# Attention weights times values on one core: the tile context is closed and compiled inside the kernel, and the wait for the last stores stands behind its closing barriers

## The chip, the cores and the metric

The kernel runs on one core of a Trainium2 chip. The metric is the device time of one execution in microseconds (us), as the median of several runs. A second source is the profile of one execution: it gives a span (from the first to the last instruction of the program) and every instruction's and transfer's time in it.

## The reference

```python
def setup_inputs():
    batch, n_heads, seq, head_dim = 8, 12, 1024, 64
    return {
        "attn_weights": np.random.randn(batch, n_heads, seq, seq).astype(np.float32),
        "v": np.random.randn(batch, n_heads, seq, head_dim).astype(np.float32),
    }

def reference(attn_weights, v):
    return np.einsum('bhqs,bhsd->bhqd', attn_weights, v).astype(np.float32)
```

There are 96 heads. For each, a 1024x1024 matrix of weights is multiplied with a 1024x64 matrix of values.

## The kernel before, in words

The 96 heads are taken four at a time, which makes `NV` = 24 groups (`q`), and each group is done in two units, so `NU` = 48 units (`n`). One unit holds 16 rows of weights per partition: the 128 partitions are four heads times 32 blocks of rows.

The steps of a unit, each on its engine, are written out by hand in one critical section with semaphores of their own:

- GpSimd (POOL) issues the load of a unit's weights, 4 MB of them, into one of two buffers `abf`; the transfer casts to bf16. It also loads `v`, several groups at once, and issues most of the stores (`load_attn`, `load_v`, `store`).
- TensorE (PE) transposes the weights (`transpose_g`, line 143), spreads the values over the partitions (`spread_v`, line 160), multiplies (`multiply`, line 188) and transposes the product back (`transpose_back`, line 173).
- VectorE (DVE) and ScalarE (ACT) copy the results of these steps from PSUM (lines 249, 257, 276 and 288). The finished rows go into `osb`, a ring of slots in SBUF from which they are stored.
- SyncE (SP) passes on semaphores and issues the last three stores.

The stores are grouped. Those of the first groups go out in two bursts (`BURSTS`). From `HELD_FROM` = 14 on, POOL holds two stores of 2 MB back until all loads are issued; they count on `s_held`. SP issues three more of 2 MB (`q` = 18, 20 and 22 from `BY_SYNC` = 18 on), which count on `s_end`; each adds 16 when it has landed, 48 in all.

How the program ends is what matters here. Inside the critical section ScalarE waits for `s_held`, and POOL closes its own list with a drain (line 402). The section's own end (line 135) lets all engines go on once POOL is through. Behind it, still inside the tile context, ScalarE waits for `s_end` (lines 433 and 434):

```python
        landed = nc.scalar.alloc_register("landed")
        nc.scalar.reg_mov(landed, 16 * (NV - BY_SYNC) // 2)
    tc.keep_in_program_order(nc.scalar.wait_ge(s_end, nc.scalar.snap(landed)))
    tc.keep_in_program_order(nc.scalar.sem_inc(s_end, 1))
```

When the `with` block of the tile context is left (line 460), the context is closed and compiled, and its closing is appended to every engine's list: a barrier of all five engines, POOL's clear of all the context's semaphores as one range, and a second barrier. In a barrier each engine drains and counts itself on one semaphore; POOL waits until the other four have done so (it gathers) and then lets them go through another semaphore (it releases).

Of the kernel before, what the change touches and what calls it, by code (L numbers as in the profile page):

```python
# [10 lines left out]
def kernel(  # L11
# [18 lines left out]
    nc = tc.nc  # L30
# [18 lines left out]
    NV = NH // VH  # L49
# [4 lines left out]
    BY_SYNC = NV - 6  # L54
# [37 lines left out]
    PER_DVE = sum(on_dve(g) for g in range(G))  # L92
    PER_ACT = G - PER_DVE

    sem = tc.alloc_semaphore
    sb = lambda name, shape, dt: nc.alloc_sbuf_tensor(name, shape, dt).ap()
    ident = sb("ident", [P, P], fp32)
# [18 lines left out]
    s_second = {n: sem(f"s_second{n}") for n in range(HALVED, NU)}  # L116
    s_v0, s_v, s_cast = sem("s_v0"), sem("s_v"), sem("s_cast")
    s_osb = sem("s_osb")
    s_held, s_end = sem("s_held"), sem("s_end")

    s_t = {True: sem("s_t_dve"), False: sem("s_t_act")}
    s_sp, s_m = sem("s_sp"), sem("s_m")
# [12 lines left out]
    with tc.tile_critical(sync_engine=mybir.EngineType.Pool, no_gpsimd_drain=True):  # L135
# [218 lines left out]
        def store(q, fours, eng, done, ready=None):  # L354
            eng.wait_ge(s_out, ready or 2 * (q + fours) + 1)
            at_slot = osb[:, ds(slot(q), fours // 2)].rearrange("p n r d -> p n (r d)")
            eng.dma_start(  # L357
                out=out_n(q, fours), in_=at_slot,
                **({"single_packet": True} if eng is pool and fours == 2 else {}),
            ).then_inc(done, 16)  # L360
# [67 lines left out]
            store(q, 2, nc.sync, s_end)  # L428
        nc.sync.wait_ge(s_fin, 2)
        store(NV - 2, 2, nc.sync, s_end, NU)  # L430
        landed = nc.scalar.alloc_register("landed")
        nc.scalar.reg_mov(landed, 16 * (NV - BY_SYNC) // 2)
    tc.keep_in_program_order(nc.scalar.wait_ge(s_end, nc.scalar.snap(landed)))
    tc.keep_in_program_order(nc.scalar.sem_inc(s_end, 1))


# [28 lines left out]
```

## Time and profile before

| what | value |
|---|---|
| time, median of 3 runs | 1051.74 us (1051.55 to 1052.11) |
| span of the profiled execution | 1049.7 us |
| time less span | 2.04 us |
| moved between HBM and the core | 427.82 MB read, 25.17 MB written |
| busy share of the span | PE 76%, DVE 37%, ACT 45%, POOL 4% |

The profile has no time of its own for the whole execution beside the span, so the profiled execution is set against the median of the runs by the 2.04 us that lie outside the span. In the profile, lines named PE, DVE, ACT and POOL are work of the engines; ACTq, DVEq, POOLq, PEldq and SPq are their sequencers, which execute semaphore instructions, drains, register moves and branches. For a group of instructions of one line it gives the duration in ns (least, median and most), and the start of the first and of the last of them in us from the start of the span. "DMA to landing" is the time from the issue of a transfer until its last part has counted on its semaphore.

### The profile page before, as it was taken

The page shows a single profiled execution, that of the slowest core. Times are in us where ns is not written, and L with a number is a line of the kernel's source. Part 1 is how long each engine was busy: PE and PEld are TensorE (multiplying, and loading weights), DVE is VectorE, ACT ScalarE, POOL GpSimd, SP SyncE. Part 2 cuts the span into 40 slices and gives each one's busy share as a digit, 9 for nine tenths or more (in the row PEclk, how much of TensorE's full clock was granted, in tenths as well). Part 3 has the DMA queues.
Part 4 walks back from the last instruction along what each step waited for, and adds up shares of the span by engine and source line. Part 5 has one row for each costly group of instructions (what it writes and reads, how often), then busy time and mean ns, then how long its engine had stood idle before and what let it go on. Part 6 is the DMA issues. An engine that isn't in the chain of part 4 may idle for free.

```text
span 1049.7 us, 17364 instructions
## 1 busy us (share of the span) xinstructions
PE 799.7 (76%) x7304; PEld 712.2 (68%) x7304; DVE 389.3 (37%) x584; ACT 469.5 (45%) x590; POOL 36.9 (4%) x68
## 2 busy tenths in 40 slices
PE   0978789479789492887949879858578894988984
PEld 0777678478678482777848678647567784877874
DVE  1443344235334251343424344324224341533542
ACT  0445355345445361344535455344335443544643
POOL 1000000000000000000000000000000000000100
PEclk9989889799898796889879989889879987889997
DMA  9999999999999999999999999999999999999999
GB/s 216 225 219 219 217 211 215 220 220 217 219 219 209 216 220 380 217 219 219 206 219 220 220 217 219 207 222 215 327 233 217 219 206 219 219 220 220 209 220 390
DMA packets 10662, 239.68 MB, mean 228 GB/s; under 512 B 1056, under 2 KB 1056, under 8 KB 1184
## 3 DMA queue, kind: packets, MB, share of 16 engines
q0 software_dynamic: 10080, 232.26, 98.8%
q1 hardware_dynamic: 576, 7.34, 1.7%
q8 instruction: 3, 0.05, 0.0%
q14 instruction: 3, 0.02, 0.0%
HBM read 427.82 MB, written 25.17 MB: 432 GB/s over the span
## 4 chain that ended last, share of the span: by engine, by line
DMA 71%; PE 26%; issue 1%; POOL 1%; ACT 0%; DVE 0%; ACTq 0%; SPq 0%; POOLq 0%
DMA abf<-in_attn_weights_dram 63%; PE bank L143 22%; DMA out_dram<-osb 8%; PE bank L160 3%; PE bank L188 1%; PE bank L173 0%; POOL vr L349 0%; ACT osb L257 0%; DVE osb L257 0%; ACT vbf L249 0%; POOL abf L343 0%; ACT ot L288 0%; POOL out_dram L357 0%; ACTq L257 0%; SPq L419 0%
## 5 line engine op out<-in xcount | busy, mean ns | idle before, releaser
L143 PE MATMUL bank<-ident,abf 128*128 128x128 f32 x3072 | 432.8, 309 | 206.3 <-DMA abf<-in_attn_weights_dram 183.1
L143 PEld LDWEIGHTS bank<-ident,abf 128*128 128x128 f32 x3072 | 423.1, 212 | 218.0 <-DMA abf<-in_attn_weights_dram 190.5
L276 DVE COPY at<-bank 128x1024 bf16<-128x1024 bf16 x480 | 319.6, 688 | 399.3 <-PE bank L143 398.5
L276 ACT COPY at<-bank 128x1024 bf16<-128x1024 bf16 x288 | 287.9, 1012 | 326.1 <-PE bank L143 326.1
L188 PE MATMUL bank<-at,vbf 128*64 128x256 bf16 x3072 | 227.3, 286 | 0.0
L188 PEld LDWEIGHTS bank<-at,vbf 128*64 128x64 bf16 x3072 | 204.8, 112 | 20.0 <-issue 6.5
L257 ACT COPY osb<-bank 64x512 f32 (+1 forms) x194 | 112.4, 580 | 28.3 <-PE bank L173 25.7
L288 DVE COPY ot<-bank 128x512 f32<-128x512 f32 x48 | 33.2, 691 | 210.2 <-PE bank L188 210.2
L160 PE MATMUL bank<-vr,spread 32*128 32x512 bf16 x768 | 87.0, 375 | 0.5 <-issue 0.2
L288 ACT COPY ot<-bank 128x512 f32<-128x512 f32 x48 | 28.1, 585 | 132.1 <-PE bank L188 132.1
L173 PE MATMUL bank<-ident,ot 128*128 128x128 f32 x392 | 62.6, 312 | 29.4 <-ACT vbf L249 28.7
L173 PEld LDWEIGHTS bank<-ident,ot 128*128 128x128 f32 x392 | 51.3, 159 | 41.5 <-ACT vbf L249 40.5
L160 PEld LDWEIGHTS bank<-vr,spread 32*128 32x128 bf16 x768 | 35.2, 93 | 43.9 <-issue 1.6
L249 ACT CAST vbf<-bank 128x512 bf16<-128x512 f32 x48 | 25.8, 589 | 74.3 <-PE bank L160 74.3
L343 POOL DMA_DIRECT2D abf<-in_attn_weights_dram x50 | 26.9, 538 | 810.9 <-PE bank L143 810.0
L249 DVE CAST vbf<-bank 128x512 bf16<-128x512 f32 x48 | 30.9, 685 | 29.0 <-PE bank L160 29.0
L276 ACT ACT_TABLE_LOAD x12 | 15.4, 1283 | 6.3 <-DMA osb<-in_v_dram 6.1
L349 POOL DMA_DIRECT2D vr<-in_v_dram x6 | 4.0, 674 | 135.9 <-PE bank L160 135.9
L357 POOL DMA_DIRECT2D out_dram<-osb x5 | 3.1, 619 | 7.5 <-ACT osb L257 7.5
L257 DVE COPY osb<-bank 64x512 f32<-64x512 f32 x2 | 1.4, 689 | 3.0 <-PE bank L173 3.0
L324 DVE MEMSET ident<- 128x128 f32 x1 | 0.2, 165 | 6.1 <-DMA osb<-in_v_dram 6.1
L331 DVE CAST vr<-osb 128x1024 bf16<-128x1024 f32 x2 | 2.2, 1136 | 0.0
(9 smaller groups left out, 5.1 us busy)
## 6 DMA issues: line engine op xcount, KB each, us to landing
abf<-in_attn_weights_dram POOLq DMA_DIRECT2D x46, 4096.0 KB, 29.2
vr<-in_v_dram POOLq DMA_DIRECT2D x5, 2048.0 KB, 15.3
out_dram<-osb POOLq DMA_DIRECT2D x1, 8192.0 KB, 40.4
abf<-in_attn_weights_dram POOLq DMA_DIRECT2D x4, 2048.0 KB, 24.6
out_dram<-osb POOLq DMA_DIRECT2D x3, 2048.0 KB, 35.4
out_dram<-osb SPq DMA_DIRECT2D x3, 2048.0 KB, 13.8
out_dram<-osb POOLq DMA_DIRECT2D x1, 4096.0 KB, 42.5
osb<-in_v_dram SPq DMA_DIRECT2D x1, 1024.0 KB, 5.0
```

Source lines behind the costliest of these rows:

```text
L143: last = pe.matmul(out=pt[g % 4][:, k], lhsT=words[:, k], rhs=ident, is_transpose=True, start=(k == 0), stop=(k == KW - 1),)
L160: last = pe.matmul(out=banks[h], lhsT=spread[rows, j, ds(VB - 1 - b, P)], rhs=vr[rows, n // 2, b], start=(b == 0), stop=(b == VB - 1),)
L173: last = pe.matmul(out=px[j0 // 4][:, ds(j * P, P)], lhsT=ot[:, j0 + j], rhs=ident, is_transpose=True, start=(j == 0), stop=(j == 3),)
L188: last = pe.matmul(out=outs, lhsT=vbf[:, 2 * kw + par, h], rhs=at[:, ds(half * GH, GH), kw, ds(h * VP, VP), par], start=(n == 0), stop=(n ...
L249: copy(out=vbf[:, :, h], in_=ps.rearrange("p (k d) -> p k d", k=SB)).then_inc(s_vbf)
L257: last = copy(out=rows[ds(n // 2 % 2 * HP, HP), ds(pp * 2 * G + n % 2 * G, G)].rearrange("p (half j) d -> p j half d", half=2)[:, ds(4 * k ...
L276: ins = copy(out=at[:, g].rearrange("c k j two -> c (k j two)"), in_=bank[g % 4].bitcast(bf16),)
L288: copy(out=ot.rearrange("c j (pp h p) -> c h j pp p", pp=2, h=VH)[:, ds(2 * e, 2)], in_=po[e].rearrange("c (h j p pp) -> c h j pp p", h=2, ...
L331: last = nc.vector.tensor_copy(out=vr_first[:, 0, part], in_=v32[:, part])
L343: pool.dma_start(out=abf[n % 2][:, ds(g0, gn)].rearrange("p g s -> p (g s)"), in_=attn_q[n // 2][:, ds((n % 2 * G + g0) * S, gn * S)],).th ...
L349: pool.dma_start(out=vr[:, ds(q % V_AT_ONCE // 2, fours // 2)].rearrange("p n b x -> p n (b x)"), in_=v_n(q, fours),).then_inc(s_v, 16)
L357: eng.dma_start(out=out_n(q, fours), in_=at_slot, **({"single_packet": True} if eng is pool and fours == 2 else {}),).then_inc(done, 16)
```

## The change

`s_end` is no longer one of the tile context's semaphores but taken from the program itself, so the closing's range clear leaves it alone. The kernel closes and compiles the tile context itself as its last step but one, and so the closing stands in every engine's list there. Then ScalarE waits for the constant 48 on `s_end` and sets the semaphore back to zero. The register, its copy and the increment go. Leaving the `with` block has nothing left to do for the context.

```diff
     PER_ACT = G - PER_DVE
 
+    s_end = nc.alloc_semaphore("s_end")
     sem = tc.alloc_semaphore
...
     s_osb = sem("s_osb")
-    s_held, s_end = sem("s_held"), sem("s_end")
+    s_held = sem("s_held")
...
         nc.sync.wait_ge(s_fin, 2)
         store(NV - 2, 2, nc.sync, s_end, NU)
-        landed = nc.scalar.alloc_register("landed")
-        nc.scalar.reg_mov(landed, 16 * (NV - BY_SYNC) // 2)
-    tc.keep_in_program_order(nc.scalar.wait_ge(s_end, nc.scalar.snap(landed)))
-    tc.keep_in_program_order(nc.scalar.sem_inc(s_end, 1))
+    tc.close()
+    tc.compile()
+    nc.scalar.wait_ge(s_end, 16 * (NV - BY_SYNC) // 2)
+    nc.scalar.sem_clear(s_end)
```

## The prediction

> **What bounds the kernel now.** I read the page first, from the span down to the chain of waits, then the last 26 us in stretches, then line by line the instructions that end the program.
>
> ```profile
> span 1049.7 us, 17364 instructions
> ...
> DMA  9999999999999999999999999999999999999999
> ...
> HBM read 427.82 MB, written 25.17 MB: 432 GB/s over the span
> ...
> DMA 71%; PE 26%; issue 1%; POOL 1%; ACT 0%; DVE 0%; ACTq 0%; SPq 0%; POOLq 0%
> ```
>
> The DMA engines are 90% busy or more in each of the 40 slices and 71% of the chain that ended last is DMA. The kernel is bound by its transfers from end to end, so an edit outside the transfers can only count at the two ends of the span. The change touches the last end. The table by stretches shows it:
>
> ```profile
> core 0: us, PE busy (x) PEld busy (x) DVE busy (x) ACT busy (x) POOL busy (x), PEclk, DMA share, GB/s
> 1024.00:1037.30 13.30, 11.20 (x121) 10.41 (x119) 6.89 (x11) 8.16 (x12) 0.00 (x0) 1.00 1.00 429
> 1037.30:1042.70 5.40, 0.00 (x0) 0.00 (x0) 0.00 (x0) 0.00 (x0) 0.00 (x0) 0.54 1.02 434
> 1042.70:1048.60 5.90, 0.00 (x0) 0.00 (x0) 0.00 (x0) 0.00 (x0) 0.00 (x0) 0.50 0.78 333
> 1048.60:1049.70 1.10, 0.00 (x0) 0.00 (x0) 0.00 (x0) 0.00 (x0) 0.00 (x0) 0.50 0.00 0
> ```
>
> Compute is over at 1037.3. From there to 1048.6 only stores move, and in the last 1.1 us not even those: no engine is busy and no byte flows. What these 1.1 us are is the whole question. The instructions of three lines tell it, first the last store and who waits for it:
>
> ```profile
> L357 SPq DMA_DIRECT2D out_dram<-osb x1: 332/332/332, 1037.3 to 1037.3; - x1
> ...
> DMA to landing us min/median/max: 11.3/11.3/11.3
> ```
>
> ```profile
> L434 ACTq EVENT_SEMAPHORE  x1: 17/17/17, 1048.7 to 1048.7; - x1
> ```
>
> The last of SP's three stores is issued at 1037.3 and lands 11.3 us later, at 1048.6. ScalarE's wait (line 434) starts to execute at 1048.7, once that has landed, and takes 17 ns. The closing of the tile context is line 460; here are its instructions before the landing and after it, in two windows:
>
> ```profile
> L460 SPq EVENT_SEMAPHORE  x3: 17/27/28, 1042.8 to 1043.0; - x3
> L460 SPq DRAIN  x2: 7/7/7, 1043.0 to 1043.1; - x2
> ...
> L460 POOLq DRAIN  x1: 47/47/47, 1043.1 to 1043.1; - x1
> ```
>
> ```profile
> L460 POOLq EVENT_SEMAPHORE  x4: 17/17/17, 1048.8 to 1049.6; - x4
> L460 ACTq DRAIN  x2: 8/8/8, 1048.7 to 1049.0; - x2
> ...
> L460 PEldq EVENT_SEMAPHORE  x2: 51/51/51, 1048.9 to 1049.6; - x2
> L460 POOLq DRAIN  x2: 39/85/131, 1048.9 to 1049.4; - x2
> ...
> L460 POOLq EVENT_SEMAPHORE_RANGE_CLEAR  x1: 268/268/268, 1049.1 to 1049.1; - x1
> ```
>
> SP and POOL reach the first closing barrier at 1043.1 and stand there. ScalarE is the fifth, and it comes only at 1048.7, with its drain behind the wait of line 434. Then the closing runs in the open: POOL gathers (1048.8), releases (PE leaves at 1048.9), drains, clears the range of semaphores (268 ns from 1049.1), drains, gathers and releases again, and the last engine leaves at 1049.6 plus 51 ns, which is the span's end.
>
> **The change part by part.** Nothing ahead of the tail is touched. The loops, the loads, the stores and the order of every queue stay; the sole new fact for the body is that one semaphore is taken outside the tile context, and the trace holds no instruction for taking one. I cost that at nothing.
>
> Removed: the register that held 48 and its copy, both on ScalarE's sequencer.
>
> ```profile
> L432 ACTq MOVE  x1: 29/29/29, 1040.1 to 1040.1; - x1
> ```
>
> ```profile
> L433 ACTq MOVE  x1: 34/34/34, 1042.8 to 1042.8; - x1
> ```
>
> They are 29 and 34 ns, at 1040.1 and 1042.8, so both lie under the 5.9 us for which ScalarE then waits for the landing. Worth nothing; without that cover they would be 0.06 us.
>
> Moved: the wait for the three stores, from ahead of both barriers to behind them. ScalarE then reaches the first barrier without it. What is late next in that barrier is POOL:
>
> ```profile
> L402 POOLq DRAIN  x1: 47343/47343/47343, 995.4 to 995.4; - x1
> ```
>
> ```profile
> L135 POOLq EVENT_SEMAPHORE  x3: 17/43/43, 1042.7 to 1043.0; - x3
> ...
> L135 ACTq DRAIN  x1: 8/8/8, 1042.8 to 1042.8; - x1
> ```
>
> POOL's drain of line 402 runs from 995.4 for 47.3 us, to 1042.7, and the critical section ends behind it, for ScalarE with a drain of 8 ns at 1042.8. POOL itself comes to the closing barrier at 1043.1 and its drain there ends at 1043.2. Behind the last arrival the closing takes what it takes now: from ScalarE's arrival at 1048.7 to 1049.7, 1.0 us. So in the changed kernel the closing runs from 1043.2 to about 1044.2. The cover is the flight of the last store, which lands at 1048.6: 4.4 us are left over. If that cover were gone (a store that landed by 1043.2), the gain would be gone with it. Behind the moved wait on ScalarE only the clear is queued, and no other engine waits for either; no DMA is issued behind it, and no queue of SP or POOL is passed by anything but the closing itself.
>
> What then ends the program is the wait at 1048.7 (17 ns, the same row of line 434 as now) and the clear behind it. Gain so far: 1049.7 - 1048.7 = 1.0 us.
>
> Added: the clear of one semaphore by ScalarE, in place of the increment that today rides on the wait. No such instruction stands in the trace. From below its price is nothing, if it is carried by the waiting instruction as the increment is. From above it is POOL's clear of a whole range, 268 ns. One semaphore is nearer to the 17 ns of ScalarE's other semaphore instructions; with the step from one instruction to the next I take 0.1 us, and keep 0 to 0.3.
>
> Around the span: the median is 1051.74 and the span 1049.7, so 2.04 us lie outside what the profile shows. Four engines are through 4.5 us sooner (at 1044.2 for 1048.7), and only ScalarE is left. Whatever of the 2.04 us these four do on their own ends up hidden; whatever ScalarE does, or all five together, stays. The bounds are 0 and -2.04 us. I take 0, by the nearest row: in the barrier of today four engines stood ready for 5.6 us, and after the fifth the closing still ran its full 1.0 us. The Trainium skill (Runtime: NRT & Kernel Launch, "The ~15µs preamble/postamble breakdown") has the work behind a kernel begin with a barrier that waits for all engines; by that rule the early four gain nothing there and the sum stays as it is. The page's stages around a kernel add up to far more than 2.04 us, so this measured time can't hold all of them, and no run so far shows which it holds.
>
> Sum: -1.0 + 0.1 = -0.9 us on the profiled span, 1049.7 to 1048.8; on the median 1051.74 to 1050.84, say **1050.8**. That is 0.09%. About 0.2%, or 2.1 us, is what a measurement of this kernel can tell from no change, so this forecast counts as "within".
>
> **The rivals.** *Four early engines shorten what lies around the span.* For it: the 2.04 us are unseen, and each engine must have some end of its own. Against it: a program isn't over before its last engine, and that one still has its own end to make. It makes the result faster by over 2.1 us once it hides more than 2.1 - 0.9 = 1.2 of the 2.04 us. With all of it hidden the time is 1050.8 - 2.0 = 1048.8; with 1.2, 1049.6. Less than that stays inside the forecast's class.
>
> *A closing drain holds until the stores have landed.* This is the one that ends slower. POOL's drain of line 402 shows that a drain can hold: the two stores it stands behind were landed when ScalarE's wait for them fired at 1040.1 (the MOVE of line 432 carries that wait), and the drain held until 1042.7, 2.6 us more. In the trace the two drains after the first barrier (131 and 39 ns) run only after the last landing; in the changed kernel they would meet two stores in flight. Should the one ahead of the clear, or SP's in the second barrier, hold in the same way, it ends at 1048.6 + 2.6 = 1051.2, then come the clear, the drain and the second barrier, 1049.7 - 1049.1 = 0.6 us, and the wait and clear, 0.1: 1051.9 for 1049.7, a time of 1053.9, slower by 2.2 us or 0.21%. It decides from a hold of about 2.5 us after the landing; a shorter one eats the gain and no more. Against it: SP's drains at 1043.0 and 1043.1 took 7 ns, and POOL's at 1043.1 took 47 ns, with SP's own store still 5 us from landing.
>
> *The move doesn't take place in the program.* If the wait were still emitted ahead of a barrier, the tail would stay as it is: 1051.7. Against it: the context is compiled on the line before, and what is traced afterwards can only follow.
>
> **How the numbers follow.** The forecast gets 0.62; its own range is 1050.4 to 1051.2: from the clear at 0 to 0.3 us (1050.7 to 1051.0), 0.2 us at the high side and 0.3 at the low for the spread of the runs (1051.55 to 1052.11) and a little hidden around the span. The early engines get 0.27: no row prices the 2.04 us, and four engines in five end sooner. The holding drain gets 0.07: drains of the same kind were seen not to hold. The wait that doesn't move gets 0.04 and counts as within. So faster 0.27, same 0.66, slower 0.07. The range goes from 1048.8, all that the first rival can give, to 1051.3, just over the forecast's own end; outside remain the drain, the unmoved wait and the stray end of a run.
>
> **What would show it.** In the changed profile the closing's instructions, whatever line they then bear, should run from about 1042.8 to 1044.2 with POOL's range clear near 1043.6; ScalarE's wait should start within 0.1 us of the last landing, 11 to 12 us after SP's last store was issued, with at most one instruction behind it; and the span should end 0.1 to 0.3 us after that landing, at about 1048.8 if the stores land as now. If the drains behind the first barrier show microseconds, the second rival is at work. If the median falls by much more than the span, it is the first. The prediction is wrong if a stretch of 1 us without transfers still stands at the end, or if the time moves by over 2 us either way.

## The result, and the profile after

The changed kernel takes 1050.42 us (median of 21 runs, 1050.12 to 1052.04) where the kernel before takes 1051.76 us (21 runs beside them). The ratio is 0.9988, with a 95% interval of 0.9982 to 0.9993: a gain of 1.3 us, or 0.12%. That is less than the 0.2% that the prediction took as the least that can be told from no change, yet the interval stays clear of 1. The profiled execution took 1050.13 us, with a span of 1048.7 us. The forecast was 1050.8.

The last 25 us in stretches, cut at the issue of the last store, at the end of the critical section and at the landing, as before. The columns are each engine's busy time, the granted clock, the share of the DMA engines and what they moved:

```profile
core 0: us, PE busy (x) PEld busy (x) DVE busy (x) ACT busy (x) POOL busy (x), PEclk, DMA share, GB/s
...
1036.90:1042.60 5.70, 0.00 (x0) 0.00 (x0) 0.00 (x0) 0.00 (x0) 0.00 (x0) 0.52 1.01 431
1042.60:1048.60 6.00, 0.00 (x0) 0.00 (x0) 0.00 (x0) 0.00 (x0) 0.00 (x0) 0.50 0.75 322
1048.60:1048.70 0.10, 0.00 (x0) 0.00 (x0) 0.00 (x0) 0.00 (x0) 0.00 (x0) 0.50 0.00 0
```

The stretch without transfers has shrunk from 1.1 us to 0.1. Where the closing went is seen in the instructions of its line, which is 433 now (the line that compiles the context), in the last 7 us:

```profile
L433 SPq EVENT_SEMAPHORE  x5: 17/17/28, 1042.8 to 1044.0; - x5
L433 POOLq EVENT_SEMAPHORE  x4: 17/17/17, 1043.1 to 1043.9; - x4
L433 SPq DRAIN  x3: 7/7/7, 1042.9 to 1043.4; - x3
L433 POOLq DRAIN  x3: 39/47/124, 1043.1 to 1043.8; - x3
...
L433 PEldq EVENT_SEMAPHORE  x2: 51/51/51, 1043.3 to 1044.0; - x2
L433 POOLq EVENT_SEMAPHORE_RANGE_CLEAR  x1: 267/267/267, 1043.5 to 1043.5; - x1
```

All of it lies between 1042.8 and 1044.0, and POOL's three drains and its range clear take what they took before, though stores are in flight. Last come the store, issued at 1036.9 with 11.7 us to its landing at 1048.6, and ScalarE:

```profile
L358 SPq DMA_DIRECT2D out_dram<-osb x1: 333/333/333, 1036.9 to 1036.9; - x1
...
DMA to landing us min/median/max: 11.7/11.7/11.7
```

```profile
L435 ACTq EVENT_SEMAPHORE_RANGE_CLEAR  x1: 41/41/41, 1048.6 to 1048.6; - x1
```

The wait of line 434 has no instruction of its own; the clear carries it and takes 41 ns.

So 1.0 us of the 1.3 is seen in the span. The rest is outside it. Every run, and not only the profiled one, lists its span beside its time, and the time less the span is steady to 0.1 us: for the kernel before 1.79 us (33 runs that were made beside the first experiments, 1.74 to 1.83), with a median span of 1050.0 us; for the changed kernel 1.47 us (21 runs, 1.41 to 1.52), with a median span of 1049.0. That is 1.0 us in the span and 0.3 around it, and the second part is what the experiments are about.

### The profile page after: what moved, and what is told of

Same layout as the page of the kernel before. It is cut to its first block, busy times and chain, and to the rows that moved or that the text cites. A ratio compares the mean times of both kernels' runs of the same rounds, so it can differ in the third digit from the quotient of the medians.

```text
span 1048.7 us, 17363 instructions
## 1 busy us (share of the span) xinstructions
PE 795.5 (76%) x7304; PEld 708.5 (68%) x7304; DVE 389.4 (37%) x584; ACT 469.5 (45%) x590; POOL 36.9 (4%) x68
## 4 chain that ended last, share of the span: by engine, by line
DMA 71%; PE 26%; issue 1%; POOL 1%; ACT 0%; DVE 0%; ACTq 0%; SPq 0%; POOLq 0%
DMA abf<-in_attn_weights_dram 63%; PE bank L144 22%; DMA out_dram<-osb 8%; PE bank L161 3%; PE bank L189 1%; PE bank L174 0%; POOL vr L350 0%; ACT osb L258 0%; DVE osb L258 0%; ACT vbf L250 0%; POOL abf L344 0%; ACT ot L289 0%; POOL out_dram L358 0%; ACTq L258 0%; SPq L420 0%
```

## The experiments

Two theories stood at the start. A: four engines that end early hide something that each does behind its last instruction. B: what lies around the span is the same in every version, and only the profiled executions differ.

**All but the move** (label e_own). The semaphore is taken from the program and cleared by ScalarE; the wait, its register and the increment stay where they were. The edit against the kernel before:

```diff
+    s_end = nc.alloc_semaphore("s_end")
...
-    s_held, s_end = sem("s_held"), sem("s_end")
+    s_held = sem("s_held")
...
     tc.keep_in_program_order(nc.scalar.wait_ge(s_end, nc.scalar.snap(landed)))
     tc.keep_in_program_order(nc.scalar.sem_inc(s_end, 1))
+    tc.keep_in_program_order(nc.scalar.sem_clear(s_end))
```

> All of the change but the move: the semaphore is taken from the program and ScalarE sets it back to zero itself, while its wait stays ahead of both closing barriers. Theory A (the gain is the 1.0 us of closing that the move hides, and about 0.4 us more around the span because four engines end early): no gain, 1051.7 to 1051.9, the span about 1.9 to 2.1 us less than the time. Theory B (what lies around the span does not depend on when the other engines end; it is about 1.5 us in every version, and the profiled execution of before was merely a shorter one): 1051.7 too, but the time less the span is 1.5 us.

Measured: 1051.85 us, ratio 0.9998 (0.9989 to 1.0007), the span 1050.1, the time less span 1.79 us (1.72 to 1.85). No gain: the move is what brings it. The closing, on line 462 in this run, stands behind the landing again:

```profile
L462 POOLq EVENT_SEMAPHORE_RANGE_CLEAR  x1: 266/266/266, 1049.6 to 1049.6; - x1
```

For the part around the span A expected too much (1.9 to 2.1 us) and B too little (1.5). Both kernels that wait ahead of the barriers, this one and the one before, have 1.79, which is 0.3 us more than the changed kernel.

**Nobody ends early** (label e_all). The closing stays early, but all engines wait for the stores behind it. This edit and those that follow are against the changed kernel.

```diff
     tc.compile()
+    done = nc.alloc_semaphore("s_done")
+    for eng in (nc.sync, nc.vector, nc.tensor, nc.gpsimd):
+        eng.wait_ge(s_end, 16 * (NV - BY_SYNC) // 2)
+        eng.sem_inc(done, 1)
     nc.scalar.wait_ge(s_end, 16 * (NV - BY_SYNC) // 2)
+    nc.scalar.wait_ge(done, 4)
     nc.scalar.sem_clear(s_end)
+    nc.scalar.sem_clear(done)
```

> The changed kernel, but the other four engines also wait for the last stores behind the closing and then count themselves on a semaphore for which ScalarE waits, so that nobody ends early. Theory A: the span is longer by 0.1 us only, 1048.8 to 1048.9 where the stores land as before, and the time less the span goes back from 1.5 to about 2.0 us: 1050.9 to 1051.0. Theory B: the time less the span stays at 1.5 us, 1050.5.

Measured: 1050.78 us, ratio 0.9988 (0.9979 to 0.9997), the span 1049.2, the time less span 1.64 us (1.57 to 1.69): between the two expectations, A's 2.0 and B's 1.5. The trace shows why it isn't the 1.79 of before. These are POOL's wait (those of SP, VectorE and TensorE start at 1048.9 too) and ScalarE's last clear:

```profile
L437 POOLq EVENT_SEMAPHORE  x1: 17/17/17, 1048.9 to 1048.9; - x1
```

```profile
L441 ACTq EVENT_SEMAPHORE_RANGE_CLEAR  x1: 41/41/41, 1049.1 to 1049.1; - x1
```

POOL is through 0.2 us ahead of ScalarE, so if POOL is the engine whose end is long, 0.2 of it is inside the span. The next two runs ask that.

**Another engine waits last.** The wait and the clear are moved to SyncE (e_sp), GpSimd (e_pool), TensorE (e_pe) and VectorE (e_dve), with the rest as in the changed kernel. The edit of e_pool:

```diff
-    nc.scalar.wait_ge(s_end, 16 * (NV - BY_SYNC) // 2)
-    nc.scalar.sem_clear(s_end)
+    nc.gpsimd.wait_ge(s_end, 16 * (NV - BY_SYNC) // 2)
+    nc.gpsimd.sem_clear(s_end)
```

> The changed kernel, but SyncE instead of ScalarE waits for the last stores and clears the semaphore. Theory A: the part around the span is that of the engine that ends last, so it may differ between engines, anywhere from 1.2 to 2.0 us: 1050.1 to 1050.9. Theory B: 1.5 us as with ScalarE, 1050.4.

> The changed kernel, but GpSimd instead of ScalarE waits for the last stores and clears the semaphore. Theory A: if GpSimd has the longest end of its own, the part around the span goes back to about 2.0 us and the time to 1050.9; with another engine as the longest it lies between 1.2 and 2.0 us. Theory B: 1.5 us, 1050.4.

After these two, theory A became C, with a constant for each engine, and the other two engines were asked, beside the changed kernel once more (e_again):

> The changed kernel once more, beside those it is compared with. Theory C (every engine has an end of its own behind its last instruction that the profile does not show: with what lies ahead of the span about 1.85 us for GpSimd, 1.47 for ScalarE, 1.30 for SyncE; the time is the latest of the engines' ends): span 1.0 us shorter than that of before, time less span 1.47 us. Rival D (the part around the span only scatters from job to job, or hangs on how many engines wait): no fixed value, anywhere between 1.3 and 1.8 us.

> The changed kernel with TensorE as the engine that waits last and clears the semaphore. Theory C: time less span is TensorE's own constant, the same within 0.1 us in every run; between 1.2 and 1.85 us, since nothing so far shows it, and not above GpSimd's, which would have shown up in the kernel before. Rival D: the scatter of 1.3 to 1.8 us within this kernel's own runs.

> The changed kernel with VectorE as the engine that waits last and clears the semaphore. Theory C: a constant of VectorE's, between 1.2 and 1.85 us, the same within 0.1 us in every run. Rival D: scatter of 1.3 to 1.8 us within its runs.

| engine that ends last | time less span, us (least to most) | median span, us | time, us | ratio to before |
|---|---|---|---|---|
| SyncE (e_sp) | 1.30 (1.26 to 1.34) | 1049.1 | 1050.39 | 0.9985 (0.9976 to 0.9994) |
| VectorE (e_dve) | 1.41 (1.36 to 1.44) | 1049.1 | 1050.51 | 0.9987 (0.9978 to 0.9996) |
| ScalarE (e_again) | 1.45 (1.42 to 1.51) | 1049.0 | 1050.51 | 0.9987 (0.9978 to 0.9996) |
| TensorE (e_pe) | 1.60 (1.53 to 1.63) | 1049.0 | 1050.60 | 0.9989 (0.9980 to 0.9998) |
| GpSimd (e_pool) | 1.83 (1.80 to 1.90) | 1049.3 | 1051.10 | 0.9993 (0.9984 to 1.0002) |
| all five (before) | 1.79 (1.74 to 1.83) | 1050.0 | 1051.81 | |

All have 11 runs, before 33. The runs were made on two chips, e_sp and e_pool on one and the other three on another; the kernel before gave 1.79 beside the first two and 1.78 beside the others. B and D fall: no row spreads over more than 0.1 us, and the part around the span goes by the engine that ends last. Only the ranges of VectorE and ScalarE overlap; SyncE, TensorE and GpSimd each stand apart. A's 2.0 us for GpSimd was too high. GpSimd's long end doesn't come from clearing the semaphore: in e_all it clears none, in the kernel before it clears none behind the last barrier, and the part around the span is long in both. The two extremes show only one instruction behind the landing, and nearly the same one:

```profile
L435 POOLq EVENT_SEMAPHORE_RANGE_CLEAR  x1: 44/44/44, 1049.0 to 1049.0; - x1
```

```profile
L435 SPq EVENT_SEMAPHORE_RANGE_CLEAR  x1: 25/25/25, 1049.0 to 1049.0; - x1
```

Both spans end at 1049.0, and the times differ by 0.5 us (1050.85 and 1050.30 in these two executions) that no instruction shows.

The constants put the other numbers together. Before, all five leave the last barrier together, POOL 0.09 us ahead of the last, and the longest end, POOL's, sets the time: 1.83 - 0.09 = 1.74 by the table, and 1.79 was measured. In e_all POOL is 0.2 us ahead of ScalarE: 1.83 - 0.2 = 1.6, and 1.64 was measured. In the changed kernel POOL ends 4.7 us ahead of ScalarE, and ScalarE's 1.47 is left: 0.3 us gained.

**More in the cover** (e_bar6 and e_bar20) **and the same in the open** (e_behind6).

```diff
     tc.compile()
+    for _ in range(6):
+        nc.all_engine_barrier()
     nc.scalar.wait_ge(s_end, 16 * (NV - BY_SYNC) // 2)
     nc.scalar.sem_clear(s_end)
```

> The changed kernel with six more barriers of all engines between the closing and ScalarE's wait. By the closing of the changed kernel one barrier takes 0.25 to 0.35 us, so six take 1.5 to 2.1 us and end near 1046, more than 2 us ahead of the last landing. Theory C with the cover of 4.6 us: no difference to the changed kernel, 1050.4, and time less span 1.47 us. Rival E (there is less cover than it seems: barriers with stores in flight are slower, or hold up the stores): 1050.9 to 1052.5.

> Twenty barriers between the closing and ScalarE's wait instead of six. In the run with six one took 0.33 us and the last one ended 2.7 us ahead of the landing, so fourteen more, 4.6 us, overrun the cover by 1.9 us. Theory C: the span is 1.9 us longer than that of the changed kernel, about 1050.9, the time less span 1.7 us since GpSimd ends nearly last again, and the time 1052.6. Rival E (barriers with stores in flight hold up the stores or are slower): more than 1053.0. Rival F (the barriers cost nothing because they never lie on the path): 1050.5.

> The same six barriers as in the kernel where they made no difference, but behind ScalarE's wait and clear. Theory C: all of them lie in the open, 6 x 0.33 = 2.0 us more span, about 1051.0, and the time less span goes to about 1.75 us since all engines end together and GpSimd's end is the longest: 1052.8. Rival F (barriers of this kind are cheap wherever they stand): 1050.5 to 1051.0.

Six in the cover: 1050.57 us beside 1050.51 for the changed kernel, time less span 1.47, and the span 1049.1. Six behind ScalarE's clear: 1052.88, ratio 1.0011 (1.0002 to 1.0020), time less span 1.80, span 1051.1. The same barriers cost nothing in one place and 2.0 us of span in the other, and there POOL's end counts again. The rows of the barriers, ahead of the wait and behind it:

```profile
L435 POOLq EVENT_SEMAPHORE  x12: 17/17/17, 1044.4 to 1046.2; - x12
```

```profile
L437 POOLq EVENT_SEMAPHORE  x12: 17/17/17, 1049.1 to 1050.8; - x12
```

Six take the same 1.7 us from the first gather to the last release, with SP's last store in flight or with none (the second of its three has landed at 1044.0, ahead of the first gather). Rival F falls.

Twenty in the cover: 1053.15 us, ratio 1.0012 (1.0003 to 1.0022), the span 1051.1, as theory C had it within 0.2. The time is 0.5 us above C's 1052.6 and in the range of rival E (more than 1053.0), but E's mechanism is not there: the last store lands 11.6 us after its issue (11.7 in the changed kernel), and a barrier takes no longer than before. The barriers run on past the landing:

```profile
L435 POOLq EVENT_SEMAPHORE  x40: 17/17/17, 1044.6 to 1050.9; - x40
```

```profile
L437 ACTq EVENT_SEMAPHORE_RANGE_CLEAR  x1: 41/41/41, 1051.1 to 1051.1; - x1
```

Where the cover ends, cost begins; that part is shown. The time less span was 2.05 us, though, where 1.7 was expected: nine of the eleven runs have 1.94 to 2.13, and two, with 1.68 and 1.71, have what C expected. One more run, with the twenty barriers behind the clear, asked whether the excess comes with the number of instructions or with the nearness of the landing:

> Twenty barriers behind ScalarE's wait and clear. With twenty ahead of it the time less span was 2.05 us where theory C had 1.7. Theory G (the length of the code that every engine has run by its end adds it): 2.05 us again, on a span of 1049.0 + 6.6 = 1055.6, so 1057.6. Theory H (it comes from ending within 2 us of the last landing): here the landing is 6.6 us past, so 1.75 to 1.8 us as with six, 1057.4.

Measured: 1057.55 us, span 1055.4, time less span 2.16 us (four runs, 2.08 to 2.21). So the nearness of the landing (theory H) falls, and the excess comes with the twenty barriers: six behind the clear leave the constant at 1.80, twenty raise it by 0.3 to 0.4, in most runs and not in all. By what they do so stays open. The traces hold one trail. Both kernels with twenty barriers show a transfer behind the last instruction, and no other trace of this case does: one packet of 8 KB on q14, which the profile calls an instruction queue. In e_bar20, from 1051 us on:

```profile
DMA packets 1, 0.01 MB, mean 1 GB/s; under 512 B 0, under 2 KB 0, under 8 KB 0
...
q14 instruction: 1, 0.01, 0.3%
```

It starts 1.9 us after the last instruction in either run and takes 0.4 us. That it causes the excess is not shown. If the measured time begins with the span, it is over 0.2 us before the packet is, and the two short runs of e_bar20 left no trace to compare.

## Why the prediction was right, and which step was off

- **The place.** Right as forecast: the closing runs from 1042.8 to 1044.0, POOL's range clear at 1043.5 (1043.6 was written), and 4.6 us of cover are left (4.4). That the cover is real, and how far it reaches, the runs with 6 and 20 barriers show.
- **The in-span gain.** 1.0 us measured, from 1049.7 to 1048.7 in the profiles and from 1050.0 to 1049.0 in the medians of the spans. The 0.1 us set aside for the clear was too much: the clear carries the wait, as the increment did, and takes 41 ns. The span's 0.9 was short by 0.1.
- **Around the span.** This is the step that was mis-sized. The prediction took 0 of the 2.04 us, arguing from the closing barrier, in which four ready engines saved nothing. It was 0.3 (1.79 to 1.47). That row says what a barrier costs behind its last arrival, and nothing of what an engine still does behind the program's last instruction. Two things lay behind that. First, 2.04 was the median of the runs less the span of one profiled execution, and that execution, with a span of 1049.7, was shorter than the median one (1050.0); taken in one and the same run it is 1.79. Secondly, the part isn't one that all engines share. Each engine has its own, from 1.30 us for SyncE to 1.83 for GpSimd, and the kernel before paid the longest.
- **The first rival** (four early engines shorten what lies around the span) was therefore the true mechanism for that part, with 0.3 us in place of the 1.2 that it needed to bring 2.1 us. Its own argument against itself, that the last engine still has its own end to make, gives the size: 1.79 - 1.47. The Trainium skill (Runtime: NRT & Kernel Launch, "The ~15µs preamble/postamble breakdown") has what follows a kernel begin with a wait until all engines are done. The runs don't speak against such a wait, since the time goes by the engine that is through last. What failed is the conclusion that the prediction drew from it, that early engines gain nothing: they gain, as far as their own end is the longer one.
- **The second rival** (a drain that holds until the stores have landed) did not happen. POOL's drains behind the first barrier took 124 and 39 ns with stores in flight (131 and 39 before, with none), and SP's 7 ns.
- **The wait that does not move** did not happen either: the only instruction behind the closing is the clear with the wait in it.

The measured 1050.4 is 0.4 lower than the forecast's 1050.8: 0.1 from the clear and 0.3 from the unseen ends. It lies at the very low end of the forecast's own range, 1050.4 to 1051.2. The 1.0 us in the span came about as worked out. By itself it gives 1050.7; the time is inside the range only because 0.3 us had been left below for the spread of the runs and a little hidden around the span, and that this was just enough is luck.

## What to carry to other kernels

A wait for the last stores belongs behind everything that doesn't need their data, the closing barriers included; what is hidden is read from the trace as the time between the last transfer's landing and the end of the span. The engine that makes this last wait should be the one with the shortest end of its own: SyncE had 1.30 us and GpSimd 1.83, 0.5 us between two lines that differ in one word. By that, SyncE is the better choice here by 0.15 us of the part around the span; its median of 1050.39 and the changed kernel's 1050.42 and 1050.51 are too close to tell them apart by the times alone. And the part of the time that lies outside the span has to be taken within one run, never as a median less another execution's span.

## What the runs showed of the hardware that was not expected

- Behind its last instruction each engine has an end that no row of the profile shows. With what lies ahead of the span, taken as the same for all because no edit adds an instruction there, it is 1.30 us for SyncE, 1.41 for VectorE, 1.45 to 1.47 for ScalarE, 1.60 for TensorE and 1.83 for GpSimd. What it consists of no run shows.
- With many more instructions it grew: 1.80 us with six added barriers behind the clear, 2.16 with twenty. The reason is open.
- A barrier of all five engines costs 0.33 us (six make 2.0), whether a store is in flight or not, and it doesn't wait for it.
- GpSimd's drain inside the critical section holds 2.6 us longer than its own stores take to land. In the changed kernel they have landed when ScalarE's branch, which carries the wait for them, starts at 1040.1 (1040.03 by their semaphore), and the drain ends at 996.5 + 46.1 = 1042.6. The distance is 2.58 us in all thirteen traces. What the drain does in it no run shows. It lies in the cover, but the closing can only start behind it.

```profile
L136 ACTq COMPARE_BRANCH  x1: 38/38/38, 1040.1 to 1040.1; - x1
```

```profile
L403 POOLq DRAIN  x1: 46118/46118/46118, 996.5 to 996.5; - x1
```
